# HGRN in a two-layer decoder trunk: log k folded into the exponent of the levels, level scores summed by three wide additions

## The chip, the cores and the metric

One core of a Trainium2 chip runs the whole kernel in one launch. The metric is the device time of one execution in microseconds; lower is better. The core has a matrix engine (TensorE, PE in the profile, with its weight loads as PEld), a vector engine (VectorE, DVE), a scalar engine for functions of one argument (ScalarE, ACT), GpSimd (POOL) and SyncE (SP), which here issues the DMAs.

## The reference

Two residual layers over 512 tokens of width 1024. The even layer has block-sparse attention, RWKV-7 time mixing and attention to memory tokens; the odd layer has differential attention, the HGRN2 gated linear recurrence and attention to memory tokens. The change touches the recurrence alone, which has 4 heads of 64 channels:

```python
def hgrn2_chunked(q, k, v, log_f):
    # q,k,log_f (B,H,S,Dk), v (B,H,S,Dv): S_t = diag(f_t) S_{t-1} + k_t v_t^T, o_t = S_t^T q_t
    def step(st, inp):
        qt, kt, vt, gt = inp
        bcum = jnp.cumsum(gt, axis=2)
        inter = jnp.einsum('bhtd,bhde->bhte', qt * jnp.exp(bcum), st)
        diff = jnp.where(causal, bcum[:, :, :, None, :] - bcum[:, :, None, :, :], NEG_INF)
        scores = jnp.einsum('bhtd,bhsd,bhtsd->bhts', qt, kt, jnp.exp(diff))
        intra = jnp.einsum('bhts,bhse->bhte', scores, vt)
        b_last = bcum[:, :, -1:, :]
        st = st * jnp.exp(b_last[:, :, 0, :])[..., None] + jnp.einsum('bhsd,bhse->bhde', kt * jnp.exp(b_last - bcum), vt)
        return st, inter + intra
```

With these inputs log_f is the log-sigmoid of the projected `fd`, and k, which is one minus f, is the sigmoid of minus `fd`.

## The kernel before, in words

Everything is fp32. Big projections are done in three passes over halves of the operands: `weights` rounds a raw weight tile to `hi` on ScalarE (L259), takes the rest `lo` on VectorE (L260), and `mm3` (L269) multiplies in groups of eight matmuls of one accumulation each. The projections of the odd layer are listed in `ODO` ("fd id qd g0 c3 ..."); each is a chunk of 256 columns.

The heads of the recurrence are done in two pairs by `hgrn_pair`, one head in each half of the 128 partitions (channels), with the 512 tokens along the free axis in four chunks of 128. From `fd` it makes `lf` (log f), `k` as the exponential of `lf - fd` (L1189, L1190), and the running sum `b` of `lf` within each chunk by a scan (L1192). The scores within a chunk are built by levels: at level hh the chunk is cut into blocks of 2 hh tokens, and a query in the later half meets a key in the earlier half. `level` makes one tile `x` for that (L1207, L1208: the exponents, against the value of `b` at the middle of the block; L1209: the exponential; L1212 and L1213: the later halves times `qd`, the earlier halves times `k`). Levels 64 and 32 are matmuls whose results ScalarE copies straight to their places in the score tile `hat` (L1224, L1237). Levels 16, 8, 4, 2, the diagonal and level 1 are 32x32 blocks in six planes: `masked` (L1245) multiplies each by its mask into `htm`, a reduction over the planes (L1271) sums them into `hsm`, and eight small copies a pair of heads (L529, on VectorE or ScalarE in turn A V V) put the blocks into `hat`. The order of the levels is `HGO`: 4 and 2, then 64, then 32, then the diagonal with 1, then 16 and 8. Last come the state: `e`, the exponential of the chunk's last `b` minus `b`, times `k` (L1275 to L1277), transposed (L1280); the states of the chunks (L1290, L1295); and the outputs, scores times values (L1300) and decayed queries times states (L1304).

The pool `dp` has one buffer for each name except `hx`, which has three, so the second pair waits for the first to be done with `hb`, `hk`, `htm` and `hsm`. Score tiles in the accumulators (`s`) have two buffers.

Nothing orders the engines by hand. Every instruction has a priority, and the builder puts together the queue of each engine before the run: of the instructions that are ready by its own estimate of time, the one of the lowest number goes first. The HGRN work has plain numbers; evacuations of projections (`band("e")`), weights (`"w"`), norms (`"n"`) and the projection matmuls (`"d"`, from 1000000 on) have later ones, so projections are put where nothing else is ready. The later matmuls of a group, once begun, go ahead of all. A queue is worked off in its order.

Of the kernel before, what the change touches and what calls it, by code (L numbers as in the profile page):

```python
# [13 lines left out]
AF = mybir.ActivationFunctionType  # L14
OP = mybir.AluOpType
AX = mybir.AxisListType
PSUM = bass.MemoryType.PSUM

P = 128
D = 1024  # L20
S = 512
NM = 256
NT = S // P
# [124 lines left out]
def tile_trunk(ctx, tc, x_in, memT_in, w_mem, e_w_in, e_w_out, o_w_in, o_w_out, ln_g, w2_in, a2_in,  # L148
# [31 lines left out]
    V, A, G = (Others(e) for e in (nc.vector, nc.scalar, nc.gpsimd))  # L180
# [6 lines left out]
    def tl(pool, shape, name, dt=F32, **kw):  # L187
        T.end()
        return pool.tile(shape, dt, tag=name, name=name, **kw)
# [3 lines left out]
    def pj(name="pj"):  # L193
        if name == "t":
            tn[0] ^= 1
            name = f"t{tn[0]}"
        T.end()
        return ps.tile([P, 512], F32, tag=name, name=name, bufs=2 if name == "pj" else 1)
# [23 lines left out]
    def C(name, j=None):  # L222
        return cst[name] if j is None else cst[name][:, j:j + 1]
# [92 lines left out]
    def col(name, n=1):  # L316
        c = sum(w for _, w in cols.values())
        cols[name] = (c, n)
        return small[:, c:c + n]
# [204 lines left out]
    def evac(dst, src, kind="d"):  # L524
        evac_n[kind] += 1
        if EVP[kind][evac_n[kind] % len(EVP[kind])] == "A":
            A.activation(dst, src, AF.Copy)  # L527
        else:
            V.tensor_copy(dst, src)  # L529
# [170 lines left out]
    with ExitStack() as ph:  # L700
# [10 lines left out]
        for h in range(2):  # L711
            t = pj("t")
# [46 lines left out]
    for n, sgn in (("aq", -0.125), ("ak", 1.0), ("cq", -0.125), ("ck", 1.0)):  # L759
        g = col("g" + n)  # L760
        tmp = col("t" + n)
# [416 lines left out]
    def hgrn_pair(dp, q, qx, fd, idn, sgd, rm128):  # L1178
        qd = qx[:, 0]
        f3 = lambda t: t.rearrange("p (c t) -> p c t", t=P)  # L1180
        e = tl(dp, [P, S], "he")
        lf = tl(dp, [P, S], "hlf")
# [2 lines left out]
        A.activation(e, e, AF.Exp, scale=-1.0)  # L1185
        A.activation(e, e, AF.Ln, bias=ones)
        V.tensor_tensor(lf, lf, e, op=OP.subtract)
        k = tl(dp, [P, S], "hk")
        V.tensor_tensor(k, lf, fd, op=OP.subtract)  # L1189
        A.activation(k, k, AF.Exp)  # L1190
        b = tl(dp, [P, S], "hb")
        V.tensor_tensor_scan(b, rm128, lf, 0.0, op0=OP.mult, op1=OP.add)  # L1192
        hs = [slice(0, 64), slice(64, 128)]
        q4 = [slice(32 * j, 32 * j + 32) for j in range(4)]
        at = [tl(dp, [P, NT, P], f"hat{p}", bufs=1) for p in range(2)]
        for p in range(2):
            G.memset(at[p], 0.0)
        tmp = [tl(dp, [P, 6, NT, 32], f"htm{p}", bufs=1) for p in range(2)]
        hl = C("hlev").rearrange("p (l t) -> p l t", t=32)

        def level(hh):
            x = tl(dp, [P, S], "hx", bufs=3)
            bv = b.rearrange("p (c z h) -> p c z h", z=2, h=hh)
            xv = x.rearrange("p (c z h) -> p c z h", z=2, h=hh)
            nb = S // (2 * hh)
            ref = bv[:, :, 0, hh - 1:hh].to_broadcast([P, nb, hh])
            V.tensor_tensor(xv[:, :, 1, :], bv[:, :, 1, :], ref, op=OP.subtract)  # L1207
            V.tensor_tensor(xv[:, :, 0, :], ref, bv[:, :, 0, :], op=OP.subtract)  # L1208
            A.activation(x, x, AF.Exp)  # L1209
            qv = qd.rearrange("p (c z h) -> p c z h", z=2, h=hh)  # L1210
            kv = k.rearrange("p (c z h) -> p c z h", z=2, h=hh)
            V.tensor_tensor(xv[:, :, 1, :], xv[:, :, 1, :], qv[:, :, 1, :], op=OP.mult)  # L1212
            V.tensor_tensor(xv[:, :, 0, :], xv[:, :, 0, :], kv[:, :, 0, :], op=OP.mult)  # L1213
            return x

        def lev64():
            x = level(64)
            s = s2()
            for p in range(2):
                for i in range(NT):  # L1220
                    T.matmul(s[0:64, p, i * 64:i * 64 + 64], x[hs[p], i * P:i * P + 64],
                             x[hs[p], i * P + 64:(i + 1) * P], start=True, stop=True)
            for p in range(2):
                A.activation(at[p][0:64, :, 64:128], s[0:64, p, 0:256].rearrange("p (i t) -> p i t", t=64), AF.Copy)  # L1224

        def lev32():
            x = level(32)
            s = s2()
            for p in range(2):
                for i in range(NT):  # L1230
                    for m in range(2):
                        o = i * P + 64 * m
                        T.matmul(s[q4[2 * m], p, i * 32:i * 32 + 32], x[hs[p], o:o + 32], x[hs[p], o + 32:o + 64],
                                 start=True, stop=True)
            for p in range(2):
                for m in range(2):
                    A.activation(at[p][q4[2 * m], :, 64 * m + 32:64 * m + 64],  # L1237
                                 s[q4[2 * m], p, 0:128].rearrange("p (i t) -> p i t", t=32), AF.Copy)
# [3 lines left out]

        def masked(s, g0):
            for p in range(2):
                V.tensor_tensor(tmp[p][:, g0:g0 + 2], s[:, p, 0:2 * P].rearrange("p (l i t) -> p l i t", l=2, t=32),  # L1245
                                hl[:, g0:g0 + 2, None, :].to_broadcast([P, 2, NT, 32]), op=OP.mult)

        def small(g0):
            s = s2()
            for l in range(2):  # L1250
                x = level(16 >> (g0 + l))
                for p, i, j, o in blocks:
                    c = l * P + i * 32
                    T.matmul(s[q4[j], p, c:c + 32], x[hs[p], o], x[hs[p], o], start=True, stop=True)
            masked(s, g0)

        def last():
            s = s2()
            A.activation(qx[:, 1], lf, AF.Exp)
            V.tensor_tensor(qx[:, 1], qx[:, 1], qd, op=OP.mult)  # L1260
            sv = s[:, :, 0:2 * P].rearrange("p a (l t) -> p a l t", t=P)
            for p, i, j, o in blocks:
                T.matmul(sv[q4[j], p, :, i * 32:i * 32 + 32], k[hs[p], o], qx[hs[p], :, o], start=True, stop=True)
            masked(s, 4)

        todo = {"A": lev64, "B": lev32, "0": lambda: small(0), "2": lambda: small(2), "4": last}
        for c in HGO:
            todo[c]()
        for p in range(2):
            sm = tl(dp, [P, NT, 32], "hsm")  # L1270
            V.tensor_reduce(sm, tmp[p].rearrange("p l i t -> p i t l"), axis=AX.X, op=OP.add)  # L1271
            for j in range(4):
                evac(at[p][q4[j], :, 32 * j:32 * j + 32], sm[q4[j]], "h")
        e = tl(dp, [P, S], "he")
        V.tensor_tensor(f3(e), f3(b)[:, :, P - 1:P].to_broadcast([P, NT, P]), f3(b), op=OP.subtract)  # L1275
        A.activation(e, e, AF.Exp)
        V.tensor_tensor(e, e, k, op=OP.mult)  # L1277
        t = pj("t")
        for i in range(NT):
            T.transpose(t[:, i * P:(i + 1) * P], e[:, i * P:(i + 1) * P], ident)  # L1280
# [34 lines left out]
        t = pj("t")  # L1315
# [61 lines left out]
    def odd_layer():  # L1377
# [6 lines left out]
        with ExitStack() as ph2:  # L1384
# [32 lines left out]
            for q in range(2):  # L1417
                hgrn_pair(dp, q, qd[q], fd[q], idn, sg[4 + q], rm128)
# [67 lines left out]
```

## Time and profile before

| what | value |
|---|---|
| median of three runs | 667.17 us (663.99 to 668.03) |
| the profiled execution | 665.84 us, of it the span 663.8 us |
| TensorE busy | 638.3 us (96%) |
| VectorE busy | 490.7 us (74%) |
| ScalarE busy | 328.7 us (50%) |
| mean granted clock of TensorE | 0.995 of full |

Busy shares are means over the whole span, and the stages have different limits; so the stretch that a change touches is read by itself. [...] An instruction's time in the order of time can overlap that of the next one on its engine. What ended an engine's idle time is inferred from the semaphores; where several were waited for, the one that came last is named.

### The profile page before, as it was taken

The page shows a single profiled execution, that of the slowest core. Times are in us where ns is not written, and L with a number is a line of the kernel's source. Part 1 is how long each engine was busy: PE and PEld are TensorE (multiplying, and loading weights), DVE is VectorE, ACT ScalarE, POOL GpSimd, SP SyncE. Part 2 cuts the span into 40 slices and gives each one's busy share as a digit, 9 for nine tenths or more (in the row PEclk, how much of TensorE's full clock was granted, in tenths as well). Part 3 has the DMA queues.
Part 4 walks back from the last instruction along what each step waited for, and adds up shares of the span by engine and source line. Part 5 has one row for each costly group of instructions (what it writes and reads, how often), then busy time and mean ns, then how long its engine had stood idle before and what let it go on. Part 6 is the DMA issues. An engine that isn't in the chain of part 4 may idle for free.

```text
span 663.8 us, 15418 instructions
## 1 busy us (share of the span) xinstructions
PE 638.3 (96%) x6192; PEld 551.6 (83%) x6192; DVE 490.7 (74%) x1394; ACT 328.7 (50%) x969; POOL 5.9 (1%) x21
## 2 busy tenths in 40 slices
PE   8899999999999999889999999999999999989997
PEld 5788878998998778557999887779999977677997
DVE  3996765879686488998747977994645657899853
ACT  5567355542230144765516585445345335767620
POOL 1000000000000000000000000000000000000000
PEclk9999999999999999999999999799999999999999
DMA  8462223222220215110424433024232331000223
GB/s 295 130 184 55 65 65 96 69 65 65 66 66 2 65 33 166 40 33 9 153 78 131 141 94 88 3 65 128 65 108 86 91 100 33 1 33 1 65 65 126
DMA packets 62905, 53.52 MB, mean 81 GB/s; under 512 B 3377, under 2 KB 61041, under 8 KB 62834
## 3 DMA queue, kind: packets, MB, share of 16 engines
q1 hardware_dynamic: 62834, 52.55, 26.1%
q8 instruction: 48, 0.79, 0.5%
q14 instruction: 23, 0.19, 0.1%
HBM read 50.44 MB, written 2.10 MB: 79 GB/s over the span
## 4 chain that ended last, share of the span: by engine, by line
PE 69%; DVE 18%; ACT 9%; issue 2%; DMA 2%; SPq 0%; ACTq 0%; DVEq 0%
PE pj L269 52%; DVE lo L260 2%; ACT pr L515 1%; ACT pr L584 1%; PE s L920 1%; PE c L914 1%; ACT hi L259 1%; PE t L1351 1%; DVE pr L513 1%; PE t L458 1%; DMA memT<-in_memT_dram 1%; DVE hsm L1271 1%; PE t L557 1%; DVE PT L529 1%; PE s L943 1%
## 5 line engine op out<-in xcount | busy, mean ns | idle before, releaser
L259 ACT ACTIVATE hi<-raw 128x512 fp32r<-128x512 f32 (+2 forms) x164 | 89.5, 597 | 80.2 <-PE pj L269 62.4
L260 DVE TENSOR_TENSOR lo<-raw,hi 128x512 fp32r<-128x512 f32 (+2 forms) x164 | 101.6, 649 | 34.1 <-PE pj L269 21.6
L269 PE MATMUL pj<-hi,act_hi 128*128 128x256 f32 x672 | 102.0, 286 | 0.2 <-DVE x L623 0.2
L269 PE MATMUL pj<-hi,act_lo 128*128 128x256 f32 x672 | 101.2, 285 | 0.6 <-DVE act_lo L311 0.6
L269 PE MATMUL pj<-lo,act_hi 128*128 128x256 f32 x672 | 100.6, 284 | 0.0
L269 PEld LDWEIGHTS pj<-hi,act_hi 128*128 128x128 f32 x672 | 88.4, 188 | 3.1 <-ACT pr L515 0.8
L269 PEld LDWEIGHTS pj<-hi,act_lo 128*128 128x128 f32 x672 | 88.4, 189 | 1.7 <-DVE act_lo L311 0.7
L269 PEld LDWEIGHTS pj<-lo,act_hi 128*128 128x128 f32 x672 | 88.1, 188 | 0.5 <-issue 0.2
L269 PE MATMUL pj<-act_hi,lo 128*128 128x512 f32 (+1 forms) x248 | 66.2, 410 | 0.0
L269 PE MATMUL pj<-act_lo,hi 128*128 128x512 f32 (+1 forms) x248 | 65.3, 406 | 0.0
L269 PE MATMUL pj<-act_hi,hi 128*128 128x512 f32 (+1 forms) x248 | 64.3, 401 | 0.2 <-ACT act_hi L461 0.2
L269 PEld LDWEIGHTS pj<-act_lo,hi 128*128 128x128 f32 (+1 forms) x248 | 46.3, 191 | 11.2
L269 PEld LDWEIGHTS pj<-act_hi,lo 128*128 128x128 f32 (+1 forms) x248 | 45.9, 191 | 10.7
L269 PEld LDWEIGHTS pj<-act_hi,hi 128*128 128x128 f32 (+1 forms) x248 | 45.1, 187 | 10.8 <-ACT act_hi L461 0.5
L623 DVE TENSOR_TENSOR x<-pj,x 128x256 f32<-128x256 f32 x64 | 27.0, 422 | 28.4 <-PE pj L269 28.3
L654 ACT ACTIVATE sq<-pj 128x64 f32<-128x64 f32 x144 | 30.0, 226 | 29.0 <-DVE nat L529 20.3
L515 ACT ACTIVATE pr<-pr,mx 128x128 f32<-128x128 f32 (+3 forms) x56 | 31.2, 561 | 12.9 <-DVE mx L513 9.0
L654 ACT ACTIVATION_READ_ACCUMULATOR sq<-pj 128x1 f32 x144 | 29.2, 212 | 0.0
L513 DVE CUSTOM_DVE_ANT_0 pr<-s,mask 128x128 f32<-128x128 f32 (+3 forms) x56 | 26.0, 483 | 1.4 <-PE t L600 1.2
L466 ACT ACTIVATE th<-pj 128x512 f32<-128x512 f32 x16 | 9.5, 597 | 31.9 <-PE pj L269 31.9
L527 ACT ACTIVATE nat<-pj 128x256 f32<-128x256 f32 (+1 forms) x17 | 6.7, 391 | 29.3 <-PE pj L269 29.3
L529 DVE COPY nat<-pj 128x256 f32<-128x256 f32 x16 | 6.7, 422 | 16.3 <-PE pj L269 16.1
(408 smaller groups left out, 1047.1 us busy)
## 6 DMA issues: line engine op xcount, KB each, us to landing
raw<-in_o_w_in_dram SPq DMA_DIRECT2D x20, 512.0 KB, 3.7
raw<-in_e_w_in_dram SPq DMA_DIRECT2D x36, 256.0 KB, 3.4
raw<-in_e_w_in_dram SPq DMA_DIRECT2D x10, 512.0 KB, 4.1
x<-in_x_dram SPq DMA_DIRECT2D x8, 512.0 KB, 6.8
raw<-in_o_w_in_dram SPq DMA_DIRECT2D x16, 256.0 KB, 3.4
raw<-in_o_w_out_dram SPq DMA_DIRECT2D x8, 512.0 KB, 3.5
raw<-in_e_w_out_dram SPq DMA_DIRECT2D x4, 512.0 KB, 3.5
raw<-in_w_mem_dram SPq DMA_DIRECT2D x4, 512.0 KB, 3.5
```

What stands on the lines that cost most here:

```text
L259: A.activation(hi[:, z, :n], r, AF.Copy)
L260: V.tensor_tensor(lo[:, z, :n], r, hi[:, z, :n].bitcast(F32), op=OP.subtract)
L269: T.matmul(o, lh(k), rh(k), start=c == 0, stop=c == tot - 1)
L458: T.transpose(t[:, k * P:(k + 1) * P], xn[i][:, (k0 + k) * P:(k0 + k + 1) * P], ident)
L466: A.activation(th, o, AF.Tanh, scale=0.5)
L513: V.tensor_tensor_reduce(pr[:, p, :n], s[:, p, :n], mask[0][:, 384 - i * P:512], 1.0, 1e38, op0=OP.add, op1=OP.min, accum_out=mx[:, p:p + 1])
L515: A.activation(pr[:, p, :n], pr[:, p, :n], AF.Exp, bias=mx[:, p:p + 1], scale=-1.0, accum_out=rs[:, p:p + 1])
L527: A.activation(dst, src, AF.Copy)
L529: V.tensor_copy(dst, src)
L557: T.matmul(o[64 * p:64 * p + 64, j * P:], v[:, j, v0 + q * P + 64 * p:v0 + q * P + 64 * p + 64], PT[p][:, 4 * j:3 * j + 4, :].rearrange("p ...
L623: V.tensor_tensor(x[i][:, cs], o, x[i][:, cs], op=OP.add)
L654: A.activation(sq[:, h0 + h], o[:, 64 * (h0 + h):64 * (h0 + h + 1)], AF.Square, accum_out=ss[:, i * nh + h:i * nh + h + 1])
```

## The change

The exponent now carries `k`. The tile `bk` first holds `lf - fd`, which is log k; `k` is made from it for the one place that still reads it, the level 1 and diagonal matmul; then `bk` becomes `b - bk`. In `level` the earlier halves take their exponent from `bk` in place of `b`, so that the exponential is already multiplied by `k`, and the multiplication L1213 goes. `e` takes its exponent from `bk` too, and L1277 goes. The two tiles `htm0` and `htm1` become one, with the same planes, and the two reductions become three additions over both heads at once, in place: three planes onto three, then one onto one twice. The copies into `hat` read the first plane.

```diff
+        bk = tl(dp, [P, S], "hbk")
+        V.tensor_tensor(bk, lf, fd, op=OP.subtract)
         k = tl(dp, [P, S], "hk")
-        V.tensor_tensor(k, lf, fd, op=OP.subtract)
-        A.activation(k, k, AF.Exp)
+        A.activation(k, bk, AF.Exp)
         b = tl(dp, [P, S], "hb")
         V.tensor_tensor_scan(b, rm128, lf, 0.0, op0=OP.mult, op1=OP.add)
+        V.tensor_tensor(bk, b, bk, op=OP.subtract)
...
-        tmp = [tl(dp, [P, 6, NT, 32], f"htm{p}", bufs=1) for p in range(2)]
+        tmp = tl(dp, [P, 2, 6, NT * 32], "htm", bufs=1)
...
+            bkv = bk.rearrange("p (c z h) -> p c z h", z=2, h=hh)
...
-            V.tensor_tensor(xv[:, :, 0, :], ref, bv[:, :, 0, :], op=OP.subtract)
+            V.tensor_tensor(xv[:, :, 0, :], ref, bkv[:, :, 0, :], op=OP.subtract)
             A.activation(x, x, AF.Exp)
             qv = qd.rearrange("p (c z h) -> p c z h", z=2, h=hh)
-            kv = k.rearrange("p (c z h) -> p c z h", z=2, h=hh)
             V.tensor_tensor(xv[:, :, 1, :], xv[:, :, 1, :], qv[:, :, 1, :], op=OP.mult)
-            V.tensor_tensor(xv[:, :, 0, :], xv[:, :, 0, :], kv[:, :, 0, :], op=OP.mult)
...
+        V.tensor_tensor(tmp[:, :, 0:3], tmp[:, :, 0:3], tmp[:, :, 3:6], op=OP.add)
+        V.tensor_tensor(tmp[:, :, 0], tmp[:, :, 0], tmp[:, :, 1], op=OP.add)
+        V.tensor_tensor(tmp[:, :, 0], tmp[:, :, 0], tmp[:, :, 2], op=OP.add)
         for p in range(2):
-            sm = tl(dp, [P, NT, 32], "hsm")
-            V.tensor_reduce(sm, tmp[p].rearrange("p l i t -> p i t l"), axis=AX.X, op=OP.add)
+            sm = tmp[:, p, 0].rearrange("p (i t) -> p i t", t=32)
             for j in range(4):
                 evac(at[p][q4[j], :, 32 * j:32 * j + 32], sm[q4[j]], "h")
         e = tl(dp, [P, S], "he")
-        V.tensor_tensor(f3(e), f3(b)[:, :, P - 1:P].to_broadcast([P, NT, P]), f3(b), op=OP.subtract)
+        V.tensor_tensor(f3(e), f3(b)[:, :, P - 1:P].to_broadcast([P, NT, P]), f3(bk), op=OP.subtract)
         A.activation(e, e, AF.Exp)
-        V.tensor_tensor(e, e, k, op=OP.mult)
```

## Rows read from the trace of the kernel before

**Rows 1.** The page's first part: busy us, share of the span, instructions.

```profile
PE 638.3 (96%) x6192; PEld 551.6 (83%) x6192; DVE 490.7 (74%) x1394; ACT 328.7 (50%) x969; POOL 5.9 (1%) x21
```

**Rows 2.** Busy time by stretches of 10 us, all engines.

```profile
core 0: us, PE busy (x) PEld busy (x) DVE busy (x) ACT busy (x) POOL busy (x), PEclk, DMA share, GB/s
...
410.00:420.00 10.00, 8.68 (x244) 6.97 (x244) 9.87 (x24) 7.37 (x17) 0.00 (x0) 0.83 0.01 3
420.00:430.00 10.00, 8.86 (x171) 7.36 (x170) 9.19 (x29) 3.64 (x8) 0.98 (x2) 0.83 0.02 4
430.00:440.00 10.00, 10.00 (x272) 8.25 (x272) 8.82 (x24) 4.53 (x11) 0.00 (x0) 1.00 0.02 3
```

**Rows 3.** The chain that ended last, 340 to 560 us: start, length, what.

```profile
447.03 89.09 PE pj L269 x704
```

**Rows 4.** TensorE's waits, 380 to 450 us: us in total, times, longest.

```profile
PE s L1300 <- DVE hat L529: 1.5, 2, 1.0
PE s L1254 <- ACT hat L1237: 1.3, 1, 1.3
PE s L1300 <- ACT hx L1209: 1.1, 1, 1.1
PE t L1280 <- DVE he L1277: 0.3, 1, 0.3
```

**Rows 5.** Busy time by stretches of 2 us, columns as in rows 2.

```profile
416.00:418.00 2.00, 2.00 (x5) 1.61 (x6) 2.00 (x7) 1.85 (x4) 0.00 (x0) 0.50 0.00 0
...
426.00:428.00 2.00, 2.00 (x61) 1.74 (x48) 1.47 (x5) 0.93 (x2) 0.00 (x0) 0.50 0.03 8
```

**Rows 6.** Order of time on TensorE: start, length, line, form, count.

```profile
415.79 3.63 PE L269 MATMUL pj<-act_hi,lo 128*128 128x512 f32 x8
419.26 2.03 PE L269 MATMUL pj<-act_hi,hi 128*128 128x512 f32 x8
...
426.68 3.33 PE L269 MATMUL pj<-act_lo,hi 128*128 128x512 f32 x8
```

**Rows 7.** Order of time on VectorE, 375 to 450 us.

```profile
379.84 0.17 DVE L238 SCALAR_TENSOR_TENSOR nw<-nw 128x8 f32<-128x8 f32 x1
380.04 0.17 DVE L239 SCALAR_TENSOR_TENSOR ksr<-nw,ksr 128x8 f32<-128x8 f32 x1
...
391.01 1.47 DVE L1213 TENSOR_TENSOR hx<-hx,hk 128x256 f32<-128x256 f32 x3
...
405.89 0.69 DVE L529 COPY qd<-pj 128x512 f32<-128x512 f32 x1 [1.47 <-PE pj L269]
...
408.23 0.69 DVE L1286 TENSOR_TENSOR hqh<-qd,heb 128x512 f32<-128x512 f32 x1
408.83 0.42 DVE L1207 TENSOR_TENSOR hx<-hb 128x256 f32<-128x256 f32 x1
409.17 0.42 DVE L1208 TENSOR_TENSOR hx<-hb 128x256 f32<-128x256 f32 x1
```

**Rows 8.** Groups by form on VectorE, 400 to 450 us: busy, mean ns | idle.

```profile
L1271 DVE TENSOR_REDUCE hsm<-htm 128x128 f32<-128x768 f32 x4 | 6.1, 1514 | 0.1
...
L529 DVE COPY hat<-hsm 32x128 f32<-32x128 f32 x11 | 2.4, 217 | 0.2
```

**Rows 9.** Order of time on VectorE at the second pair's sums.

```profile
440.10 1.52 DVE L1271 TENSOR_REDUCE hsm<-htm 128x128 f32<-128x768 f32 x1
...
442.80 1.55 DVE L1271 TENSOR_REDUCE hsm<-htm 128x128 f32<-128x768 f32 x1
444.45 0.68 DVE L529 COPY hat<-hsm 32x128 f32<-32x128 f32 x3
```

**Rows 10.** Order of time on VectorE: the second pair's scan.

```profile
413.15 1.22 DVE L1192 TENSOR_TENSOR_SCAN hb<-rm,hlf 128x512 f32<-128x512 f32 x1
```

**Rows 11.** Order of time on ScalarE around the second pair's start.

```profile
414.50 0.63 ACT L1284 ACTIVATE heb<-hb 128x512 f32<-128x512 f32 x1
...
416.72 0.63 ACT L1190 ACTIVATE hk<-hk 128x512 f32<-128x512 f32 x1
```

More of the change, by code (lines that the diff above doesn't have):

```diff
@@ L1244, in masked @@
             for p in range(2):
-                V.tensor_tensor(tmp[p][:, g0:g0 + 2], s[:, p, 0:2 * P].rearrange("p (l i t) -> p l i t", l=2, t=32),
+                V.tensor_tensor(tmp[:, p, g0:g0 + 2].rearrange("p l (i t) -> p l i t", t=32), s[:, p, 0:2 * P].rearrange("p (l i t) -> p l i t", l=2, t=32),
                                 hl[:, g0:g0 + 2, None, :].to_broadcast([P, 2, NT, 32]), op=OP.mult)
```

## The prediction

> **What bounds the kernel now.** I read the page's first part, then the busy time by stretches, then the waits of TensorE in the stretch that the change touches, and last the order of time on each engine there. The first view shows TensorE busy for 638.3 of 663.8 us and VectorE for 490.7 [rows 1]. On the whole this is a TensorE kernel, and the change neither adds nor removes a matrix multiplication. It can therefore only pay by TensorE's standing still, or running slowly, beside the HGRN work.
>
> That work lies between about 382 and 447 us. In it VectorE is the full engine: 9.87 of 10 us from 410 to 420, 9.19 from 420 to 430, while TensorE has gaps: 8.68 and 8.86 of 10 [rows 2]. The chain that ended last also shows where the stretch ends: from 447.03 on it is 89.09 us of projection matmuls and nothing else [rows 3], so whatever TensorE wins before 447 is carried on, and work after it gains nothing by itself.
>
> TensorE's waits in 380 to 450 us sum to 4.2 us [rows 4]: 1.5 for the copies into `hat` behind the second pair's reductions, 1.3 for ScalarE's copies into `hat` (they free a score buffer), 1.1 at the first pair's output matmuls, 0.3 for `e` times `k`. [...]
>
> **The change part by part.** On VectorE an instruction of 128x512 starts 0.60 us and one of 128x256 0.34 us before the next, though they last 0.69 and 0.42: independent ones overlap. One that needs the result of the one before it does not: the short steps of the root start every 0.20 us though each lasts 0.17 [rows 7]. I take the last as its duration plus 0.03.
>
> Multiplying by `k` at L1213 goes, six times a pair, 12 in all: 12 x 0.34 = 4.1 us of VectorE. In the first pair three of the six ran from 391.01 on, while `qd` came only with the copy at 405.89 [rows 7], so only nine of them (3.0 us) lie in the full stretch.
>
> Multiplying `e` by `k` (L1277) goes, two instructions of the size 128x512, 0.60 us each; the new subtraction `b - bk` has the same form, so the two balance at 0. The first of the two removed ones held TensorE for 0.3 us [rows 4], so its going is worth that on the path, if the exponential before it is not later. The subtraction that fed `k` is kept under another name.
>
> The sums change form. Before, two reductions a pair of 768 elements, 1.51 us each [rows 8]. After, one addition of 768 and two of 256, each waiting for the one before. The page has no addition of 768; from 0.42 us for 256 and 0.69 for 512 the line gives 0.95. With 0.03 between them: 0.95 + 0.42 + 0.42 + 0.09 = 1.9 us, against 3.0. That is 1.1 us less a pair. The bounds: if the wide addition cost what the reduction of the same width costs (1.51), 0.5 is left; if the additions overlapped like independent ones (0.87 + 0.34 + 0.34), 1.5. I take 1.1, since the two widths of the same instruction are nearest.
>
> [...]
>
> The order at the end changes too. Now the second reduction waits for the copies that read the first one's result, for both write one buffer `hsm`: in the second pair the reductions start at 440.10 and 442.80 and the last three copies start at 444.45 and last 0.68 [rows 9]: 5.0 us from the first reduction to the last copy, and the first pair has the same pattern. After: 1.9 us of additions, then 8 copies of which 5 or 6 are VectorE's at 0.23 us, 1.2 in all [rows 8]: 3.1 us, or 3.7 if one of the weight subtractions (0.60) is still put between. So `hat` is whole 1.3 to 1.9 us sooner after the last mask. Against it stands that the first half of `hat` can't come before the second any more; but the output matmuls ask for both halves at once, and only two of the sixteen ran ahead now.
>
> All in all VectorE has 3.0 + 2 x 1.1 = 5.2 us less in the full stretch. What TensorE gets of it, wait by wait: the 0.3 at `e` goes whole. The 1.3 for ScalarE's copies is set by ScalarE's own queue; that queue starts on an exponential of which one VectorE multiplication stands ahead, so 0.3 comes back and 1.0 stays. The 1.1 at the first pair's output goes nearly whole, for `hat` and the exponential named with it both come at least 1.1 us earlier (1.0 for its own three multiplications, and the additions): 1.1. Of the 1.5 at the second pair's output about half comes back, 0.8: the copies come 1.3 to 1.9 us sooner, but TensorE will also have less filler between, the next weights being just converted there. Sum 0.3 + 0.3 + 1.1 + 0.8 = 2.5 us. I count nothing for the clock, for the small matmuls that stand ahead of both slow groups remain, and one of the two waits as well.
>
> The added wait: `bk` is written twice, and the second writing, `b - bk`, must wait until ScalarE has made `k` from the first. In the first pair this costs nothing that is seen: TensorE has its projections, and the levels stand for `qd` anyway. In the second pair the scan starts at 413.15 and lasts 1.22 [rows 10], and ScalarE's exponential of `k` starts at 416.72 and lasts 0.63, behind that of `b` at 414.50 and the conversion of weights [rows 11]. So the price of the wait lies between nothing, if the exponential moves forward, and 417.35 - 414.37 = 3.0 us, if it stays and VectorE comes to the subtraction right behind the scan. I take nothing: `k` of the second pair had to wait for the last L1213 of the first pair to free its buffer, and that reader is gone; and each queue is put in order anew at build time, by what is ready. Behind the subtraction VectorE would hold the last level, the masks and the sums of the first pair, and TensorE's score matmuls wait for these.
>
> **The sum.** The profiled execution took 665.84 us, of which 663.8 is the span; less 2.5 gives 663.3. It ran 1.3 us faster than the median of the runs, 667.17, so on the median's footing the time is 664.7.
>
> **The rivals.**
> [...]
>
> Second, hidden anyway: projections are ordered ahead of the output matmuls at other places, or the buffers of `hx` and the scores set the pace, so that TensorE finds other waits of the same length. Then only the 0.3 at `e` and 0.3 at ScalarE remain: 666.6. For it speaks that 5 us of VectorE time sit beside only 4.2 us of waits, spread over four causes.
>
> [...]
>
> That the change doesn't do what it says, the additions costing as much as the reductions, has its bound above: 0.5 instead of 1.1 us a pair, which takes some 0.6 us from the forecast and is inside its range.
>
> **How the numbers follow.** The forecast, 662.5 to 666, gets 0.48; the full return 0.17, hidden anyway 0.20, slower 0.15. The runs before spread from 663.99 to 668.03, so 1% (6.7 us) is about what a measurement here can tell from no change. Faster by over 1% means under 660.5: most of the full return and nothing else, 0.13. Slower by over 1% means over 673.8: more than the third rival gives, so only if such a stall comes in several places, 0.05. The rest, 0.82, is within 1%. The range reaches from 659.3, a little beyond the full return, to 669.8, a little beyond the slower rival, leaving some 0.15 to 0.2 for a queue order that nothing here shows.
>
> **What would show it.** In the changed profile: three additions a pair at 0.95, 0.42 and 0.42 us where the reductions stood; no multiplication by `hk` on VectorE; VectorE busy about 5 us less between 406 and 447; the wait for `he` gone; waits of TensorE in this stretch near 1.7 instead of 4.2 us; still two stretches of granted clock at 0.50; and the long run of projections starting 2 to 3 us earlier than 447.03. It is wrong if VectorE stands idle ahead of the new subtraction for over a microsecond, if the clock drops a third time or not at all, or if the run of projections after the HGRN stretch gets a gap of its own.

## The result and the profile after

The changed kernel has a median of 663.08 us (18 runs, 661.90 to 665.33) beside 667.03 for the kernel before (18 runs, 663.99 to 668.91): a ratio of 0.9949, 95% interval 0.9935 to 0.9964. By the medians 3.95 us are gained, by the ratio 3.4 (0.0051 x 667.03), where 2.5 were forecast. The profiled execution took 663.54 us with a span of 661.7, against 665.84 and 663.8, so the two traces show 2.1 us of it. Five runs at a far lower mean clock (four of the kernel before at 0.85, one of e_first at 0.56) are left out of all medians and ratios here.

The page's first part of the changed kernel, busy us, share and instructions [rows 1]:

```profile
PE 637.9 (96%) x6192; PEld 551.2 (83%) x6192; DVE 484.2 (73%) x1384; ACT 329.5 (50%) x969; POOL 6.0 (1%) x21
```

VectorE has 6.5 us less in the whole span. From 404 to 450 us it went from 40.76 to 35.62 us busy: 5.1 less, and 5.2 were forecast. From 406 to 447 us, the window that the prediction names, it is 38.54 and 34.81, 3.7 less, for in the kernel before more of VectorE's other work falls behind it (1.7 us from 447 to 450, now 0.3).

TensorE's waits from 380 to 450 us, columns as in [rows 4]:

```profile
PE s L1255 <- ACT hat L1238: 1.1, 1, 1.1
PE t L1282 <- ACT he L1279: 1.1, 1, 1.1
PE s L1234 <- DVE nw L241: 0.6, 1, 0.6
PE t L1292 <- DVE idn L529: 0.6, 1, 0.6
PE s L1255 <- issue: 0.3, 1, 0.3
```

Set beside [rows 4]: both waits at the output matmuls (1.5 and 1.1) are gone, no line with L1302 is left. ScalarE's copies have 1.1 for 1.3. But the wait for `e` grew from 0.3 to 1.1, and three new small ones came (0.6, 0.6, 0.3). The sum went only from 4.2 to 3.7.

The changed kernel's order of time on TensorE [rows 6]:

```profile
416.00 0.59 PE L1255 MATMUL s<-hx 64*32 64x32 f32 x44 [1.13 <-ACT hat L1238]
416.87 0.95 PE L1255 MATMUL s<-hx 64*32 64x32 f32 x84 [0.28 <-issue]
417.75 3.69 PE L269 MATMUL pj<-act_hi,lo 128*128 128x512 f32 x8
421.27 2.03 PE L269 MATMUL pj<-act_hi,hi 128*128 128x512 f32 x8
423.14 2.03 PE L269 MATMUL pj<-act_lo,hi 128*128 128x512 f32 x8
425.01 1.89 PE L1302 MATMUL s<-idn,hat 128*128 128x64 f32 x16
...
430.21 2.12 PE L269 MATMUL pj<-act_hi,lo 128*128 128x512 f32 x8
...
441.87 2.08 PE L1302 MATMUL s<-idn,hat 128*128 128x64 f32 x16
444.80 1.12 PE L269 MATMUL pj<-hi,act_lo 128*128 128x256 f32 x8
```

Its busy time by stretches of 2 us [rows 5]:

```profile
418.00:420.00 2.00, 2.00 (x5) 1.55 (x6) 2.00 (x7) 1.32 (x3) 0.00 (x0) 0.50 0.04 12
...
426.00:428.00 2.00, 2.00 (x61) 1.86 (x61) 1.94 (x5) 0.86 (x2) 0.99 (x2) 1.00 0.03 8
```

Of the two stretches at a granted clock of 0.50 the first remains (the group of 3.69 us, in [rows 6] 3.63). The second is gone: the stretch 426 to 428 has a granted clock of 1.00 where [rows 5] has 0.50, and the next projection group, at 430.21, takes 2.12 us where the one at 426.68 of [rows 6] took 3.33. All sixteen output matmuls of each pair stand in one piece with no wait before them. The second of the projection groups after the HGRN work (`hi` times `act_lo`) starts at 444.80 us, in the kernel before at 446.84:

```profile
446.84 1.20 PE L269 MATMUL pj<-hi,act_lo 128*128 128x256 f32 x8
```

That is 2.0 us earlier, nearly the whole difference of the spans (2.1). Hardly anything is won or lost after that.

The new additions, and the second writing of `bk`, in order of time on VectorE:

```profile
389.63 0.69 DVE L1194 TENSOR_TENSOR hbk<-hb,hbk 128x512 f32<-128x512 f32 x1 [0.57 <-ACT hk L1191]
...
417.68 0.69 DVE L1194 TENSOR_TENSOR hbk<-hb,hbk 128x512 f32<-128x512 f32 x1 [0.19 <-ACT hk L1191]
...
438.83 0.96 DVE L1270 TENSOR_TENSOR htm<-htm 128x768 f32<-128x768 f32 x1
439.82 0.42 DVE L1271 TENSOR_TENSOR htm<-htm 128x256 f32<-128x256 f32 x1
440.28 0.43 DVE L1272 TENSOR_TENSOR htm<-htm 128x256 f32<-128x256 f32 x1
440.81 1.16 DVE L529 COPY hat<-htm 32x128 f32<-32x128 f32 x5
```

From the first addition to VectorE's last copy it is 3.1 us (438.83 to 441.97), to ScalarE's last one 3.3, where [rows 9] had 5.0. The level matmuls ahead of these sums start at 436.70 us, in the kernel before at 436.64; `hat` is whole at 442.10, before at 445.13. So in the second pair `hat` comes 3.0 us sooner: 1.3 of it lie before the first sum, 1.8 in the sums and copies.

In the first pair it is otherwise. VectorE's last copies there, before and after:

```profile
422.41 0.68 DVE L529 COPY hat<-hsm 32x128 f32<-32x128 f32 x3
```

```profile
423.11 1.39 DVE L529 COPY hat<-htm 32x128 f32<-32x128 f32 x6
```

`hat` is whole at 423.09 before and at 424.50 after, 1.4 us later. The stage itself starts 1.65 us later (its first level matmuls at 407.66 and 409.31), most of which TensorE lost at the longer waits for `e` and `idn` ahead of it (0.8 and 0.6). So measured from there `hat` comes only 0.2 us sooner: other VectorE work stands between the additions, with a wait of 0.52 us for `qd`. What took the wait away is the queue: three projection groups now stand ahead of the output matmuls (417.75, 421.27, 423.14) where two stood before (415.79, 419.26 in [rows 6]). Had there been two again, TensorE would have come at 423.14 and waited some 1.4 us, by my estimate from these times.

The executions of one program differ in TensorE's mean granted clock over the span. For the changed kernel it was 1.0 in 8 of 18 runs (spans 660.1 to 661.2) and 0.996 or 0.997 in the other 10 (660.8 to 662.7); for the kernel before, of 83 runs beside the experiments, 0.997 in 16 (median span 662.9), 0.995 in 36 (664.8), 0.992 in 18 (665.8), and never 1.0. At 0.997 the spans are 662.9 before and 661.6 after (medians of 16 and of 6): by this estimate 1.3 us lie in holes and order. The rest of the 3.4, some 2 us, goes with the clock: the changed kernel runs less of its time at a granted clock below 1.00.

### The profile page after: what moved, and what is told of

It reads as the page before. It is cut to its first block, busy times and chain, and to the rows that moved or that the text cites. A ratio compares the mean times of both kernels' runs of the same rounds, so it can differ in the third digit from the quotient of the medians.

```text
span 661.7 us, 15396 instructions
## 1 busy us (share of the span) xinstructions
PE 637.9 (96%) x6192; PEld 551.2 (83%) x6192; DVE 484.2 (73%) x1384; ACT 329.5 (50%) x969; POOL 6.0 (1%) x21
## 4 chain that ended last, share of the span: by engine, by line
PE 71%; DVE 15%; ACT 10%; issue 2%; DMA 2%; SPq 0%; ACTq 0%; DVEq 0%
PE pj L269 54%; ACT hi L259 1%; DVE lo L260 1%; ACT pr L584 1%; ACT pr L515 1%; PE s L920 1%; PE c L914 1%; PE t L1353 1%; DVE pr L513 1%; PE t L458 1%; DMA memT<-in_memT_dram 1%; PE t L557 1%; DVE PT L529 1%; PE s L943 1%; DVE mmx L581 1%
```

## The experiments

The theory to be tried, A: the sums come sooner, so `hat` is whole when TensorE comes to the output matmuls, its two holes there close, and the stretch at a granted clock of 0.50 behind them goes. The rival, B: the gain is VectorE's smaller load (the multiplications by `k`), wherever the sums stand. Two smaller questions are the price of the wait on `bk` and what holds `e`. Each kernel has 5 to 12 runs, taken in three sets beside the kernel before, whose medians were 666.95, 667.20 and 666.75. "At 0.997" is the median span of the runs with that mean clock (for split32 0.996), 2 to 7 of each kernel, which takes most of the clock's share out; for the kernel before it is 662.9 (662.5 to 663.3 by sets), after the change 661.6. Differences of less than 1 us in that column tell nothing by themselves.

| run | median us | ratio to before, 95% | at 0.997 |
|---|---|---|---|
| adds | 664.05 | 0.9958 (0.9944 to 0.9972) | 662.2 |
| fold | 668.26 | 1.0019 (1.0002 to 1.0036) | 664.0 |
| hsm2 | 664.08 | 0.9960 (0.9948 to 0.9972) | 662.4 |
| bk2 | 663.00 | 0.9940 (0.9928 to 0.9952) | 661.0 |
| fold_hsm2 | 668.24 | 1.0015 (0.9995 to 1.0034) | 664.2 |
| e_by_k | 666.48 | 0.9986 (0.9966 to 1.0006) | 662.7 |
| split32 | 666.13 | 0.9991 (0.9969 to 1.0013) | 663.6 |
| bk2_split32 | 665.74 | 0.9974 (0.9956 to 0.9993) | 663.4 |
| planes_inner | 666.05 | 1.0003 (0.9975 to 1.0031) | 661.7 |
| load_back | 664.48 | 0.9981 (0.9956 to 1.0006) | 662.0 |
| e_first | 662.41 | 0.9935 (0.9917 to 0.9953) | 661.2 |
| copies_rotated | 664.26 | 0.9962 (0.9943 to 0.9981) | 661.7 |

**adds**: the kernel before with the three additions and the one `htm`, without the fold.

```diff
...
+        V.tensor_tensor(tmp[:, :, 0:3], tmp[:, :, 0:3], tmp[:, :, 3:6], op=OP.add)
+        V.tensor_tensor(tmp[:, :, 0], tmp[:, :, 0], tmp[:, :, 1], op=OP.add)
+        V.tensor_tensor(tmp[:, :, 0], tmp[:, :, 0], tmp[:, :, 2], op=OP.add)
         for p in range(2):
-            sm = tl(dp, [P, NT, 32], "hsm")
-            V.tensor_reduce(sm, tmp[p].rearrange("p l i t -> p i t l"), axis=AX.X, op=OP.add)
+            sm = tmp[:, p, 0].rearrange("p (i t) -> p i t", t=32)
```

> The kernel before with only the three additions in place of the reductions; k is still multiplied in. [...] Theory B (VectorE is the full engine, so the six multiplications a pair, 4.1 us, carry the gain): at most 1 us faster. Theory C (every microsecond of VectorE counts alike, 2.2 of 5.2): about 1.4 us faster.

Measured: 0.9958, 3.0 us by the medians. TensorE's waits from 375 to 452 us in adds:

```profile
PE s L1254 <- ACT hat L1237: 1.8, 2, 1.3
PE s L1254 <- issue: 1.5, 1, 1.5
...
PE s L1302 <- DVE hat L529: 0.2, 1, 0.2
```

At the outputs 0.2 us are left of 2.6, with all twelve multiplications by `k` in place. So the edit of the sums is enough to close the two holes, as A says. That the sums' own speed closes them is not shown. In the first pair three projection groups stand ahead of the outputs, as after the change; `hat` is whole at 422.75, and after two groups TensorE would have come at 420.53, 2.2 us too early by this estimate. In the second pair TensorE comes late: it has just lost 1.5 us at the hole put down to "issue", and the granted clock is 0.63 and 0.52 from 438 to 442 us. Every kernel here with the additions has three groups ahead of the first pair's outputs, and every one with reductions has two.

**fold**: the changed kernel with the two reductions and the two `htm` put back (the diff of adds, the other way round); the fold stays.

> The changed kernel with the reductions put back: only log k in the exponent. Theory A: within 1 us of before, the waits at the output matmuls still there (1 us and more each), and the wait for e longer than before, near 1.1 us. Theory B: 2 to 3 us faster than before. Theory C: about 2 us faster.

Measured: 1.0019, no faster than the kernel before (by its interval a hair slower) though VectorE does less, 486.4 us for 490.7. TensorE's waits in fold, from 375 to 452 us:

```profile
PE s L1300 <- DVE hat L529: 1.6, 1, 1.6
PE s L1255 <- ACT hat L1238: 1.4, 2, 1.1
PE s L1300 <- ACT hx L1212: 1.0, 1, 1.0
```

The order of time on TensorE in fold around the first pair's outputs:

```profile
420.04 2.04 PE L269 MATMUL pj<-act_hi,hi 128*128 128x512 f32 x8
423.05 0.41 PE L1300 MATMUL s<-idn,hat 128*128 128x64 f32 x2 [0.97 <-ACT hx L1212]
...
425.82 2.97 PE L1300 MATMUL s<-idn,hat 128*128 128x64 f32 x14 [1.58 <-DVE hat L529]
428.72 1.55 PE L1304 MATMUL s<-hst,hqh 64*128 64x64 f32 x12
...
431.18 3.78 PE L269 MATMUL pj<-act_lo,hi 128*128 128x512 f32 x8
```

Busy time by stretches of 2 us in fold, columns as in [rows 2]:

```profile
426.00:428.00 2.00, 2.00 (x12) 2.00 (x11) 2.00 (x5) 0.63 (x1) 0.00 (x0) 0.53 0.01 4
...
434.00:436.00 2.00, 2.00 (x17) 1.35 (x16) 0.84 (x4) 0.00 (x0) 0.00 (x0) 0.50 0.00 0
```

In fold only two projection groups stand ahead of the outputs; TensorE waits twice in front of them (0.97 and 1.58 us), with nothing but small matmuls between and after, and then has a granted clock of 0.50 to 0.53 from 426 to 436. B falls: less load without the earlier sums is no gain. The effects also don't add up: by the medians the additions change the time by -3.0 us, the fold by +1.2, both together by -3.95.

**hsm2** and **fold_hsm2**: the two reductions freed from each other by a second buffer, in the kernel before and in fold.

```diff
-            sm = tl(dp, [P, NT, 32], "hsm")
+            sm = tl(dp, [P, NT, 32], "hsm", bufs=2)
```

> The kernel before with two buffers for hsm, so that the second reduction need not wait for the copies of the first; nothing else. If the way from the last mask to the last copy is what TensorE pays for, some 0.5 to 1 us of the 5.0 us from the first reduction to the last copy goes, and the kernel is 0.5 to 1 us faster. If TensorE's holes there are set by the order of its own queue, no change.

> The fold with the reductions and two buffers for hsm: the changed kernel but for the three additions. The theory so far (the sums cost TensorE through the shared buffer hsm, not through their length): as fast as the kernel with two hsm buffers alone or as the changed one, 663 to 664.5 us, and about 3 to 4 us faster than the fold alone. If it is the cheaper additions that make the fold harmless (1.1 us less of VectorE a pair), it stays near 666 to 668 us.

Measured: hsm2 has 0.9960, as much as adds, with the slow reductions kept: they now follow each other (2.92 us for both) and the copies come together behind them, so that the waits at the outputs are 1.0 and 0.5. Two groups still stand ahead of the first pair's outputs, so here `hat` itself comes sooner, whole at 422.31 us and 1.0 sooner measured from the stage's start. For the kernel before the shared buffer was thus as good a place to cut as the reductions' time. But fold_hsm2 has 1.0015, no better than fold: TensorE again comes after two projection groups and waits for `hat`, 2.7 us in four pieces. So neither the buffer nor the kind of sum is the cause by itself. What counts is when `hat` is there as measured by the place that the outputs have in TensorE's queue, and that place moves with the edit.

**planes_inner**: fold_hsm2 with `htm` stored with the six planes innermost. The queues of TensorE, ScalarE, GpSimd and SyncE are the same as in fold_hsm2, so that only durations on VectorE differ.

```diff
-        tmp = [tl(dp, [P, 6, NT, 32], f"htm{p}", bufs=1) for p in range(2)]
+        tmp = [tl(dp, [P, NT, 32, 6], f"htm{p}", bufs=1) for p in range(2)]
...
-            V.tensor_reduce(sm, tmp[p].rearrange("p l i t -> p i t l"), axis=AX.X, op=OP.add)
+            V.tensor_reduce(sm, tmp[p], axis=AX.X, op=OP.add)
```

> The fold with reductions and two hsm buffers as before, but the six planes lie innermost in htm, so that the reduction reads neighbours and the masks write every sixth element; TensorE's and ScalarE's queues are the same, instruction by instruction. If the reduction's 1.51 us come from reading planes 512 bytes apart and TensorE's wait for hat comes from that, the reductions take about 0.95 us, hat comes 1.1 us sooner, the wait of 1.65 us at the first pair's output falls to about 0.5 and the kernel goes from 668.2 to 665 to 667 us. If the reduction is slow in itself, nothing changes (668.2, within 1 us).

Groups by form on VectorE in planes_inner, 400 to 452 us, columns as in [rows 8]:

```profile
L1246 DVE TENSOR_TENSOR htm<-s,chlev 128x256 f32<-128x256 f32 x12 | 6.7, 641 | 1.0 <-PE s L1255 1.0
L1272 DVE TENSOR_REDUCE hsm<-htm 128x128 f32<-128x768 f32 x4 | 3.6, 935 | 0.0
```

The first pair's outputs in order of time on TensorE in fold_hsm2:

```profile
422.95 0.41 PE L1300 MATMUL s<-idn,hat 128*128 128x64 f32 x2 [1.65 <-DVE hat L529]
423.66 1.75 PE L1300 MATMUL s<-idn,hat 128*128 128x64 f32 x14 [0.31 <-DVE hat L529]
...
426.56 2.16 PE L1255 MATMUL s<-hx 64*32 64x32 f32 x128
```

The same in planes_inner:

```profile
422.13 0.33 PE L1300 MATMUL s<-idn,hat 128*128 128x64 f32 x2
422.68 1.75 PE L1300 MATMUL s<-idn,hat 128*128 128x64 f32 x14 [0.22 <-DVE hat L529]
...
425.17 1.30 PE L1255 MATMUL s<-hx 64*32 64x32 f32 x126
```

With the queue held fixed, reductions of 0.94 instead of 1.51 us bring the copies 1.0 us forward (they start at 421.14, in fold_hsm2 at 422.13) and the waits for `hat` at the outputs go from 2.7 us to 0.2. Part of that is chance: a stretch at a granted clock of 0.50 and 0.64 (416 to 420 us) fell ahead of the outputs in this execution and not in that of fold_hsm2 (1.00 there), so TensorE came 0.8 us later (422.13 against 422.95 - 1.65 = 421.30). The 32-column matmuls behind keep a granted clock of 1.00 (1.30 us where fold_hsm2 has 2.16 at 0.50). In time, the medians differ by 2.2 us and the spans at 0.997 by 2.5 (of 2 and 3 runs), but the intervals of the two ratios overlap, and five runs of planes_inner had a clock of 0.992. So the trace shows the wait closing; that the time follows is not settled.

**copies_rotated**: the kernel before with the copies into `hat` dealt out V A V instead of A V V, the same work in another order.

```diff
-EVP = {'d': 'VA', 't': 'AV', 'c': 'A', 'h': 'AVV'}
+EVP = {'d': 'VA', 't': 'AV', 'c': 'A', 'h': 'VAV'}
```

> The kernel before with the copies into hat shared out V A V instead of A V V: the same work in nearly the same order, a control for what a small shift in the queues does by itself. If times of this kernel depend only on the work, 667.0 within 0.5 us. If the arrival of hat and the clock behind it decide, up to 2 us to either side.

Measured: 0.9962, as much as adds. The order of time on TensorE in copies_rotated:

```profile
415.43 3.66 PE L269 MATMUL pj<-act_hi,lo 128*128 128x512 f32 x8
...
420.81 0.33 PE L1300 MATMUL s<-idn,hat 128*128 128x64 f32 x2
421.06 0.76 PE L1254 MATMUL s<-hx 64*32 64x32 f32 x64
421.75 2.14 PE L269 MATMUL pj<-act_lo,hi 128*128 128x512 f32 x8
423.73 1.67 PE L1300 MATMUL s<-idn,hat 128*128 128x64 f32 x14
```

The builder put one projection group between the first two output matmuls and the other fourteen. That covers the first pair's wait with the same reductions, and the second stretch at a granted clock of 0.50 does not come (1.00 from 420 to 448). The second pair's wait stays (1.1 us in all at the outputs). So a gain of this size needs no faster sums: it is to be had from the order alone.

**load_back**: the changed kernel with a maximum of the tile with itself, which changes no value, where each multiplication by `k` stood; VectorE's load is as before, the sums are the new ones.

```diff
             V.tensor_tensor(xv[:, :, 1, :], xv[:, :, 1, :], qv[:, :, 1, :], op=OP.mult)
+            V.tensor_tensor(xv[:, :, 0, :], xv[:, :, 0, :], xv[:, :, 0, :], op=OP.max)
```

> The changed kernel with VectorE's load put back: after each level's multiplication by q a maximum of the earlier halves with themselves, which changes no value, stands where the multiplication by k stood (12 more instructions of 128x256, 4.1 us). If VectorE's time as such is what the change saved, 2 to 4 us slower than the changed kernel. If only the arrival of hat at TensorE's output matmuls counts, within 1 us of the three additions alone (664.1), for it is that kernel but for where k is multiplied in.

Measured: 664.48 us, near adds. It is above the changed kernel by 1.4 us by the medians, 2.1 by the ratios and 0.4 by the span at 0.997; the two intervals overlap (0.9956 to 1.0006 beside 0.9935 to 0.9964). No wait for `hat` came back at the outputs, where again three groups stand ahead. What the load of 12 multiplications is worth by itself stays open.

**bk2**, **e_by_k**, **e_first** ask after `bk` and `e`. bk2 writes `b - bk` to a tile of its own, so it needn't wait for `k`; e_by_k makes `e` from `b` and multiplies by `k` as before; e_first makes the first pair's `e` ahead of its levels (`make_e` holds the three lines that make it).

```diff
-        V.tensor_tensor(bk, b, bk, op=OP.subtract)
+        lk, bk = bk, tl(dp, [P, S], "hbk2")
+        V.tensor_tensor(bk, b, lk, op=OP.subtract)
```

```diff
-        V.tensor_tensor(f3(e), f3(b)[:, :, P - 1:P].to_broadcast([P, NT, P]), f3(bk), op=OP.subtract)
+        V.tensor_tensor(f3(e), f3(b)[:, :, P - 1:P].to_broadcast([P, NT, P]), f3(b), op=OP.subtract)
         A.activation(e, e, AF.Exp)
+        V.tensor_tensor(e, e, k, op=OP.mult)
```

```diff
         V.tensor_tensor(bk, b, bk, op=OP.subtract)
+        if not q:
+            make_e()
...
-        e = tl(dp, [P, S], "he")
-        V.tensor_tensor(f3(e), f3(b)[:, :, P - 1:P].to_broadcast([P, NT, P]), f3(bk), op=OP.subtract)
-        A.activation(e, e, AF.Exp)
+        if q:
+            make_e()
```

> The changed kernel with b - bk written to a tile of its own, so that this subtraction no longer waits for ScalarE's exponential of k. If that wait is what moved e's exponential back (TensorE waits 1.1 us for e in the changed kernel, 0.3 before), e comes some 0.8 us sooner and the kernel is 0.5 to 1 us faster than the changed one. If ScalarE's order of work holds e back, the wait on e stays near 1.1 us and the time stays as with the change, within 0.3 us.

> The changed kernel, but e takes its exponent from b again and is multiplied by k on VectorE. If the wait for e (1.1 us in the changed kernel against 0.3 before) comes from bk being late, it goes back to 0.3 and the kernel is 0.5 to 0.8 us faster than the changed one. If it comes from the order of ScalarE's queue, where three conversions of weights and three exponentials stand ahead of e, the wait stays near 1 us or grows by the multiplication, and the time is the same or up to 0.5 us longer.

> The changed kernel with the first pair's e made ahead of the levels. If ScalarE's queue order is what holds e (1.1 us of TensorE's time), the wait goes and the kernel is about 1 us faster than the changed one, 662.0. If what TensorE wins there is only lost again at the next wait, 663.1 as before.

Measured: bk2 has 0.9940, not to be told from the changed kernel, and the wait for `e` is still 0.9 us there. In e_by_k that wait stays at 1.1, and it is 3.4 us slower than the changed kernel by the medians (its interval begins at 0.9966, above 0.9964): in its profile there is a hole of 1.5 us among the second pair's small matmuls and a stretch at a granted clock of 0.50 to 0.54 from 438 to 444 behind it. In e_first the wait shrinks to 0.3 us, but 0.4 come at the next step (`hkh`); it has 0.9935, 0.7 us by the medians below the changed kernel, which the intervals don't tell apart. It has the lowest median of all versions.

The three were made to ask why `e` is late in the changed kernel. The two traces show that it isn't later than before. The kernel before, its exponential, its multiplication by `k` and its transposes on TensorE:

```profile
393.17 0.63 ACT L1276 ACTIVATE he<-he 128x512 f32<-128x512 f32 x1
393.93 0.69 DVE L1277 TENSOR_TENSOR he<-he,hk 128x512 f32<-128x512 f32 x1
394.77 0.63 PE L1280 MATMUL t<-cident,he 128*128 128x128 f32 x4 [0.33 <-DVE he L1277]
```

The changed kernel:

```profile
393.14 0.62 ACT L1279 ACTIVATE he<-he 128x512 f32<-128x512 f32 x1
393.82 0.66 PE L1282 MATMUL t<-cident,he 128*128 128x128 f32 x4 [1.09 <-ACT he L1279]
```

The exponential starts at the same time, behind three conversions of weights and three exponentials of levels in both, and without the multiplication `e` is whole 0.9 us sooner (393.76 for 394.62). But TensorE comes 1.7 us sooner (392.73 for 394.44): six projection groups of 256 columns stand between the `kn` transposes and these in its queue, where eight stood before (in e_by_k seven, in e_first five). So the wait grew because the place in TensorE's queue moved further than `e` did. What e_first shows beside it is that moving `e` ahead in ScalarE's queue shortens the wait.

**split32** and **bk2_split32**: in the changed kernel and in bk2, half of level 32's copies into `hat` (m = 1) go to VectorE, to shorten ScalarE's 1.1 us; `dst` and `src` are the two operands of the copy.

```diff
-                    A.activation(at[p][q4[2 * m], :, 64 * m + 32:64 * m + 64],
-                                 s[q4[2 * m], p, 0:128].rearrange("p (i t) -> p i t", t=32), AF.Copy)
...
+                    if m:
+                        V.tensor_copy(dst, src)
+                    else:
+                        A.activation(dst, src, AF.Copy)
```

> The changed kernel with half of level 32's four copies into hat on VectorE instead of all on ScalarE. [...]

> Both: b - bk in a tile of its own and half of level 32's copies on VectorE. Own tile alone gave 663.0 us, no different from the changed kernel at 663.1. If the two are independent, this takes the time of the kernel with the split copies alone, within 0.5 us.

Measured: neither gained. split32 is 3.1 us slower than the changed kernel by the medians, bk2_split32 2.7 slower than bk2 and 0.4 faster than split32. The wait only changed hands (in split32 1.9 us for VectorE's copies, two times), the wait for `e` came twice (2.6 us), and other holes came with the new order.

## Why the prediction came out as it did

The forecast held in sign and lies within 2 us of the result: 664.7 forecast, 663.08 measured. The gain was 2.5 by the forecast, 3.4 by the ratio. But the mechanism held only in part, and that the number lies so near is in part luck: in the profiled pair TensorE's waits gave back 0.5 us where the sum had 2.5, and the clock, at nothing in the sum, gave 1.3. The terms, in its order:

- **VectorE's share was right.** Forecast 0.95, 0.42 and 0.42 for the additions, measured 0.96, 0.42 and 0.43; 5.2 us less in the stretch, measured 5.1; over the whole span its rows give 4.1 + 2 x 1.1 = 6.3, measured 6.5.
- **The reduction's 1.51 us** [rows 8] is the price of reading the six planes 512 bytes apart: in planes_inner, where they lie side by side, it takes 0.935 us, near the 0.96 of the wide addition. The layout moves the cost, though: the masks' products, now written in steps of 24 bytes, took 0.64 us where they took 0.42.
- **The outputs: 1.9 forecast, 2.6 measured.** The first pair's 1.1 went, but not as said: the prediction has `hat` come at least 1.1 us earlier, and it came 1.4 us later by the clock of the trace, 0.2 sooner measured from the stage's start; a third projection group ahead of the outputs covers it. That term came true by luck. In the second pair `hat` did come sooner, by 1.8 us in the sums and copies, as said (1.3 to 1.9), and by 3.0 with what VectorE has less ahead of them, and all of the 1.5 went and not about half. adds shows that the edit of the sums is enough; copies_rotated shows that another order alone can do as much, and no run parts the two in the changed kernel.
- **ScalarE's copies: 0.3 forecast, 0.2 measured.**
- **The wait for `e`: forecast gone, measured 1.1.** The prediction tied it to a condition, "if the exponential before it is not later". It was not later (393.14 us for 393.17), and `e` was whole 0.9 us sooner. The term still has the wrong sign, 0.8 us lost where 0.3 were to be won, for it took the place of the transposes in TensorE's queue as fixed, and they stand two projection groups earlier. The prediction knew that each queue is put in order anew, but counted that only for the wait on `bk`.
- **The added wait on `bk`: price 0 forecast, none found.** VectorE stands 0.57 and 0.19 us there, and bk2, without the wait, is not to be told from the changed kernel. The 3.0 us at the upper end of its price did not come.
- **New holes** of 0.6, 0.6 and 0.3 us were not in the sum; "TensorE finds other waits of the same length", from the hidden rival, holds for these.
- **The clock: 0 forecast, some 2 us measured.** This is the term that was mis-sized, "I count nothing for the clock". In the profiled pair the second slow group lost 1.3 us before (3.33 us beside the 2.03 of the group at 419.26 [rows 6]) and none after (2.12 us at a clock of 1.00). Over the runs, the mean clock of the changed kernel is 0.996 to 1.0 and that of the kernel before 0.989 to 0.997 in all but one. The prediction kept both stretches, "for the small matmuls that stand ahead of both slow groups remain, and one of the two waits as well". But the traces show a clock of 1.00 behind those same matmuls where no wait stands among them (426 to 430 in the changed kernel and in copies_rotated), and in adds even behind the first wait (stretch 416 to 420).
- **The full return (chance 0.17) and slower (0.15)**, which set the ends of the range: no run of the changed kernel shows either; its times lie between 661.90 and 665.33 us. In their place its profile shows waits of 3.7 us left, one group at a granted clock of 0.50 (3.69 us) and no third one.

So the wins at the outputs and at ScalarE's copies (2.6 + 0.2) less the new waits (0.8 + 1.5) leave 0.5 us of holes between the traces, and the slow stretch 1.3: together 1.8 of the 2.1. Over the runs the clock has the larger part, about 2 of 3.4 by the estimate above.

Of the prediction's own signs, three did not come: the wait for `he` is not gone, the waits are 3.7 and not near 1.7 us, and one stretch at a clock of 0.50 is left and not two. VectorE's 5 us less came from 404 to 450, but only 3.7 between 406 and 447. The additions' times, the missing multiplications and the earlier run of projections (2.0 us) came as said.

**Open.** The hole put down to "issue" (1.5 us in adds and e_by_k, 1.7 in load_back, 0.3 after the change) waits for nothing that the profile shows; in the three it falls at the same place of TensorE's order, after 4544 or 4545 matmuls. Its cause is not known; it stands in the profiles of some of these kernels and not of others, so it is also among what blurs the comparison. Why the first slow stretch comes in some executions of a program and not in others wasn't found, nor why the builder puts two projection groups ahead of the first pair's outputs with reductions and three with additions. So it stays open how much of the gain belongs to sooner sums and how much to the new order.

## What to carry to other kernels

Where a full matrix engine works off a fixed queue, ask of each of its waits when the input is there, measured against the place that the wait has in the queue; the load of the other engine says little by itself. Before half a per cent is credited to an edit, run one that only shuffles the order: here edits that only moved copies between engines shifted the time by 2.5 us down (copies_rotated, by the ratio) and 3 us up (split32, by the medians). Look behind every hole among small matmuls for a stretch of lower granted clock, for closing the hole can give back as much again there (1.3 us behind a hole of 1.1, in the kernel before), and a large matmul group put between did it here as well as a faster producer (copies_rotated, clock 1.00 from 420 to 448).

## What the runs showed of the hardware

- A hole of 1.1 to 1.6 us among matmuls of 32 to 64 columns was followed in several traces by a granted clock of 0.50 for 2 to 10 us: 416 to 418 in copies_rotated behind 1.33 us (0.75 in the next 2 us), 426 to 436 in fold behind 1.58 (0.53 in the first 2 us). The same hole was not followed by it in another (1.32 us in adds, clock 1.00 from 416 to 438). 8 of 18 runs of the changed kernel had a mean clock of 1.0 over the whole span, the others 0.996 or 0.997.
- On VectorE the reduction over six planes takes 1.51 us with the planes 512 bytes apart (fold_hsm2) and 0.935 with them side by side (planes_inner); a product of 256 elements takes 0.42 us written densely and 0.64 in steps of 24 bytes (the same two runs).
